# Eight early pairs of MLP blocks instead of four, their two first products kept in DRAM instead of PSUM

## The chip, the cores and the metric

The kernel runs on one core of one Trainium2 chip. TensorE (PE in the profile) multiplies, VectorE (DVE), ScalarE (ACT) and GpSimd (POOL) work element by element, and SyncE (SP) here only issues DMAs; ACT and POOL issue DMAs too. Each engine works through its own queue in the order in which the built program has it. The metric is the device time of one execution in microseconds (us). A kernel is run several times, and the median counts; beside it there is one profiled execution, from which all rows below come.

## The reference

The program is one layer of a decoder on 512 tokens of width 2048, in float32: a norm, a token mixer of four kinds of heads, a residual, a second norm, and a squared-ReLU MLP with a hidden width of 8192, a residual, and a last norm. The change is in the second norm and in the first half of the MLP:

```python
def _sq_relu_mlp(h, w_up, w_down):
    return jnp.square(jax.nn.relu(h @ w_up)) @ w_down

    for l in range(DEPTH):
        ...
        m = _rmsnorm(h, norm2_w[l])
        h = h + _sq_relu_mlp(m, w_ffn_up[l], w_ffn_down[l])
    return _rmsnorm(h, final_norm_w)
```

## The kernel before

**Precision.** A float32 operand is split into two parts (`hi`, cast to fp32r on ACT, and `lo`, the rest, subtracted on DVE), and a product is three matmuls: hi by hi, hi by lo, lo by hi. In `product` these are lines L1440, L1441 and L1442, eight times over (k = 0 to 7), 24 matmuls of 256 columns.

**The up product.** `m @ w_up` is done with a Strassen-Winograd scheme of seven products in place of eight. The activations are cut into four quarters (tokens by width), of which seven operands are made: `a11`, `a12`, `s1`, `s2`, `s3`, `s4`, `a22` (each as hi and lo, transposed). The weights are cut into 64 blocks of 128 columns, which are taken in 32 pairs. For each pair p, four pieces of 512 KB ("11", "21", "12", "22") are loaded by `load_pair`, summed as the scheme wants it (L1431), split (L1433 on ACT, L1434 on DVE, both in `prepare`), multiplied (`product`), and the seven results are put together by `combine` into a tile `ct` of eight parts, which ACT writes to DRAM as one DMA of 1 MB (L1607, `hq`, called h in the rows). There are two `ct` tiles, so the tile of pair p + 2 is the one of pair p, and its first write waits until the 1 MB of pair p has landed. `prepare` runs three products ahead of PE, and `load_pair` two pairs ahead.

**The second norm and the early products.** The operands `a11` and `a12` belong to the first half of the tokens and are there first. The other five need the norm of the second half, which DVE computes (L391, L1368 and on), and PE transposes what comes out (L1337, four transposes to a "turn", 20 turns). In that stretch PE also runs products 1 and 2 (`a11` with "11", `a12` with "21") of the first EARLY = 4 pairs: eight products, in the loop over `j`, with the 20 turns dealt out among them by `step`. `norm_second` is a generator; a `yield n` lets n steps pass, and there are eight steps to a product. Product 1 of the early pairs stays in two PSUM banks (`X`), the square of the ReLU of products 1 + 2 goes to DRAM through POOL (`e11`, L1490). The weights of these eight products are loaded and split apart from the pairs' own (L287, L280, L281), so that the early pairs' "11" and "21" are loaded twice.

**The order.** From the second norm to the end of the up product, the queues of PE and POOL are in program order, as written. The order of the other queues (DVE, ACT, SP) is set by a planner that places an instruction where it expects its inputs to be ready. `units` is the list of products after the early ones: five for an early pair (products 5, 6, 7, 3, 4), seven for any other. Every seventh unit lets POOL issue three DMAs that add weights of the down product in DRAM (L309, L310, L312, L314, tile t); that is spaced by a small copy on ACT (L309).

Of the kernel before, what the change touches and what calls it, by code (L numbers as in the profile page):

```python
# [191 lines left out]
def tile_trunk(ctx: ExitStack, tc: tile.TileContext, ins, out):  # L192
    nc = tc.nc
    V, A, PE, G = nc.vector, nc.scalar, nc.tensor, nc.gpsimd
    pool = lambda name, bufs, **kw: ctx.enter_context(tc.tile_pool(name=name, bufs=bufs, **kw))
    cp = pool("c", 1)
# [42 lines left out]

        return 8 * (p // 4) + p % 4, 8 * (p // 4) + 4 + p % 4  # L240

    EARLY = 4
    hq = [pd.tile([128, 8, 4, 256], F32, tag=f"h1_{c}", name=f"h1_{c}") for c in range(8)]
    e11 = [pd.tile([128, 256], F32, tag=f"e{p}", name=f"e{p}") for p in range(EARLY)]
    seq = [(ins["win"][b, q], 8 * len(BLOCKS[b])) for b in range(NBLK) for q in range(2)]
    seq += [(ins["wout"][n, q], 1024) for n in range(4) for q in (6, 7, 0, 1)]
    seq += 2 * [(ins["wout"][n, q], 1024) for n in range(4) for q in (4, 5, 2, 3)]
# [1108 lines left out]
    def norm_second(ss):  # L1356

        pairs = [(tt, c) for tt in range(2) for c in range(2)]
        for t in (2, 3):
            spill(t)  # L1360
        rs = [mean_rsqrt(None, ss[tt]) for tt in range(2)]
        for tt in range(2):
            for i in range(4):
                norm_i(ht[2 + tt], rs[tt], nrow2, ht[2 + tt], i)
        a11, a12, a21, a22 = ({p: ht[2 * i + p[0]][2 * j + p[1]] for p in pairs} for i in range(2) for j in range(2))
        s1 = {p: R("s1") for p in pairs}
        for p in pairs:
            V.tensor_tensor(s1[p], a21[p], a22[p], op=ALU.subtract)  # L1368
        yield 30
        for p in pairs:  # L1370
            turn("s1", s1[p], *p)
            yield 2
        ready.add("s1")
        s2 = {p: S("s2") if p in pairs[:2] else a11[p] for p in pairs}
        for p in pairs[2:]:
            V.tensor_tensor(a21[p], a11[p], a21[p], op=ALU.subtract)
        for p in pairs:
            V.tensor_tensor(s2[p], s1[p], a11[p], op=ALU.subtract)
        for p in pairs:
            yield 2  # L1380
            turn("s2", s2[p], *p)
        ready.add("s2")
        for p in pairs:
            V.tensor_tensor(a12[p], a12[p], s2[p], op=ALU.add)
        for p in pairs:
            yield 2
            turn("s4", a12[p], *p)
        for p in pairs[:2]:
            V.tensor_tensor(a21[p], a11[p], a21[p], op=ALU.subtract)
        for p in pairs:  # L1390
            yield 2
            turn("s3", a21[p], *p)
        for p in pairs:
            turn("a22", a22[p], *p)

    def pass2(th):
# [46 lines left out]
            if between:  # L1443
                between()

    def xbank(p):
        if p < EARLY:
            if p % 2 == 0:
                bank["e"] = pp.tile([128, 512], F32, tag="pp", name="x")
            return bank["e"][:, 256 * (p % 2):256 * (p % 2) + 256]  # L1450
        return pp.tile([128, 512], F32, tag="pp", name="x")[:, 0:256]

    in_order(EN.PE, EN.Pool)
    ss = pass2(0)
    operand("a11", AT)
# [11 lines left out]
        operand(name, home)  # L1467
    todo.append([norm_second(ss), 1])
    step()
    X = {}  # L1470
    ct0 = cp.tile([128, 512], F32, name="ct0")
    for j in range(2 * EARLY):
        p, m = j // 2, 1 + j % 2
        h, l = weights(2)
        if j == 2 * EARLY - 3:
            load_pair(0)
        if j >= 2 * EARLY - 3:
            prepare(j + 3 - 2 * EARLY)
# [12 lines left out]

# [74 lines left out]

    post, cts = [], {}

    def combine(p, m, acc):


        if p not in cts:
            cts[p] = pu.tile([128, 8, 256], F32, tag="ct", name="ct", bufs=2)
            if p < EARLY:
                A.copy(cts[p][:, 2], X[p])
        ct = cts[p]
        if m == 1:
            A.copy(ct[:, 2], acc)  # L1580
        elif m == 2:
            x = cts[p, 2] = pu.tile([128, 256], F32, tag="c11", name="c11", bufs=2)
            V.tensor_tensor(x, ct[:, 2], acc, op=ALU.add)
        elif m == 5:
            A.copy(ct[:, 5], acc)
        elif m == 6:
            V.tensor_tensor(ct[:, 0], ct[:, 2], acc, op=ALU.add)
# [21 lines left out]
    for u, (p, m) in enumerate(units):  # L1609
# [143 lines left out]
```

## Time and profile before

| what | us |
|---|---|
| median of 3 runs (lowest, highest) | 2385.65 (2385.21, 2393.04) |
| the profiled execution, time | 2385.64 |
| its span, first to last instruction | 2383.8 |
| PE busy in it | 2319.7 (97%) |
| DVE busy | 1773.7 (74%) |
| ACT busy | 1016.8 (43%) |
| first matmul of the early products (L1440, tile x) | 1075.3 |
| first matmul of the units (L1440, tile p) | 1120.1 |

In the rows below a time is in us from the start of the span. A row of a timeline has start, length, engine, line, operation, out<-in, how many, and in brackets how long the engine sat idle before it and what ended that. Matmuls are pipelined, so that their lengths overlap; the distance between starts is what counts. The same holds for DVE and ACT, where the next instruction starts a little before the one ahead has ended. A row of the view by stretches has the length, then busy time and count of PE, of PE's weight loads, DVE, ACT and POOL, then the granted TensorE clock, the share of the DMA engines, and GB/s.

### The profile page before, as it was taken

What the parts mean: (1) busy time and instruction counts of PE and PEld (TensorE: products, weight loads), DVE (VectorE), ACT (ScalarE), POOL (GpSimd) and SP (SyncE); (2) the same over time, 40 slices, a digit from 0 to 9 for tenths busy, and PEclk for the clock granted to TensorE, in tenths of its full rate; (3) what the DMA queues carried; (4) which work ended last, traced back from release to release, by engine and by line L of the source; (5) the groups of instructions that cost most, each with busy time, mean ns of one, the idle gap of its engine ahead of it and who ended that gap; (6) DMA issues with size and microseconds to landing.
All of it is one profiled execution on the core that took longest, in us unless ns stands there. A gap on an engine that the chain in (4) does not pass through costs nothing.

```text
span 2383.8 us, 36706 instructions
## 1 busy us (share of the span) xinstructions
PE 2319.7 (97%) x14690; PEld 1988.4 (83%) x14690; DVE 1773.7 (74%) x2783; ACT 1016.8 (43%) x1480; POOL 193.1 (8%) x270
## 2 busy tenths in 40 slices
PE   6999999999999999998999999999989999999996
PEld 6777778777777788877999999999978888888885
DVE  5685855775584444468888888888868888898898
ACT  5323233323322232354555555555555444444443
POOL 1110201211210210011011000000010000000000
PEclk9999999999999999999999999999999999999998
DMA  5553626564653676465877754445385655656451
GB/s 198 146 142 82 163 71 153 154 147 107 164 145 91 181 193 226 148 223 175 249 221 208 217 175 138 157 158 176 115 325 176 212 161 175 201 181 207 160 196 71
DMA packets 159915, 404.76 MB, mean 170 GB/s; under 512 B 12928, under 2 KB 79488, under 8 KB 158720
## 3 DMA queue, kind: packets, MB, share of 16 engines
q1 hardware_dynamic: 83952, 285.42, 36.7%
q0 software_dynamic: 38912, 77.08, 14.3%
q10 hardware_dynamic: 36880, 39.92, 4.9%
q8 instruction: 115, 1.88, 0.3%
q14 instruction: 56, 0.46, 0.1%
HBM read 355.70 MB, written 113.77 MB: 197 GB/s over the span
## 4 chain that ended last, share of the span: by engine, by line
PE 78%; DVE 10%; issue 6%; DMA 3%; POOL 1%; ACT 1%; SPq 0%; POOLq 0%; ACTq 0%; DVEq 0%
PE acc L456 17%; PE dn L1659 8%; PE dn L1658 8%; PE dn L1657 8%; PE p L1440 8%; PE p L1442 8%; PE p L1441 8%; PE wo L1238 2%; PE wo L1239 2%; PE wo L1246 2%; DVE lo L281 1%; PE acc L480 1%; DVE lo L1563 1%; DVE lo L1434 1%; DVE xi L566 1%
## 5 line engine op out<-in xcount | busy, mean ns | idle before, releaser
L1657 PE MATMUL dn<-hi,x 128*128 128x512 f32 x896 | 351.6, 392 | 11.2 <-ACT hi L1562 9.1
L1562 ACT CAST hi<-raw 128x1024 fp32r<-128x1024 f32 x224 | 235.5, 1054 | 294.9 <-PE dn L1659 233.9
L1658 PE MATMUL dn<-lo,x 128*128 128x512 f32 x896 | 351.6, 392 | 3.3 <-DVE lo L1563 3.1
L1659 PE MATMUL dn<-hi,x 128*128 128x512 f32 x896 | 351.4, 392 | 0.5 <-DVE x L1563 0.5
L280 ACT CAST hi<-raw 128x1024 fp32r<-128x1024 f32 x162 | 169.9, 1049 | 406.8 <-PE acc L456 307.2
L456 PE MATMUL acc<-ah,hi 128*128 128x512 f32 x832 | 336.4, 404 | 0.0
L456 PE MATMUL acc<-al,hi 128*128 128x512 f32 x832 | 335.4, 403 | 0.0
L456 PE MATMUL acc<-ah,lo 128*128 128x512 f32 x832 | 333.8, 401 | 0.0
L1563 DVE TENSOR_TENSOR lo<-raw,hi 128x1024 fp32r<-128x1024 f32 x224 | 272.7, 1221 | 65.7 <-ACT hi L1562 64.9
L1433 ACT CAST hi<-raw 128x1024 fp32r<-128x1024 f32 x216 | 226.3, 1050 | 209.3 <-PE p L1441 146.6
L1434 DVE TENSOR_TENSOR lo<-raw,hi 128x1024 fp32r<-128x1024 f32 x216 | 262.6, 1220 | 68.4 <-ACT hi L1433 67.8
L281 DVE TENSOR_TENSOR lo<-raw,hi 128x1024 fp32r<-128x1024 f32 x160 | 195.2, 1221 | 144.7 <-ACT hi L280 129.2
L1657 PEld LDWEIGHTS dn<-hi,x 128*128 128x128 f32 x896 | 169.7, 189 | 48.3 <-ACT hi L1562 10.4
L1658 PEld LDWEIGHTS dn<-lo,x 128*128 128x128 f32 x896 | 169.6, 189 | 40.2 <-DVE lo L1563 5.0
L1659 PEld LDWEIGHTS dn<-hi,x 128*128 128x128 f32 x896 | 169.7, 189 | 36.3 <-DVE x L1563 1.0
L456 PEld LDWEIGHTS acc<-ah,hi 128*128 128x128 f32 x832 | 156.3, 188 | 38.4 <-issue 7.4
L456 PEld LDWEIGHTS acc<-ah,lo 128*128 128x128 f32 x832 | 156.4, 188 | 34.6 <-issue 2.9
L456 PEld LDWEIGHTS acc<-al,hi 128*128 128x128 f32 x832 | 156.5, 188 | 32.0 <-issue 1.9
L1431 DVE TENSOR_TENSOR raw<-raw,raw 128x1024 f32<-128x1024 f32 x124 | 151.4, 1221 | 4.3 <-DMA raw<-in_wup_dram 2.6
L1558 DVE TENSOR_TENSOR raw<-raw 128x1024 f32<-128x1024 f32 x64 | 77.7, 1220 | 3.7 <-DMA raw<-in_wdn_dram 3.1
L310 POOL TENSOR_TENSOR pace<-pace,mhalf 128x1 f32<-128x1 f32 x64 | 37.7, 589 | 446.8 <-ACT pace L309 446.7
L1563 DVE TENSOR_TENSOR x<-raw,x 128x1024 fp32r<-128x1024 f32 x56 | 68.1, 1218 | 6.8 <-ACT x L1562 6.8
(498 smaller groups left out, 5057.2 us busy)
## 6 DMA issues: line engine op xcount, KB each, us to landing
raw<-in_wup_dram SPq DMA_DIRECT2D x136, 512.0 KB, 5.7
t<-in_wdn_dram POOLq DMA_DIRECT2D x128, 512.0 KB, 8.0
raw<-in_win_dram SPq DMA_DIRECT2D x106, 512.0 KB, 3.8
raw<-in_wdn_dram SPq DMA_DIRECT2D x96, 512.0 KB, 4.5
h<-ct ACTq DMA_DIRECT2D x32, 1024.0 KB, 9.5
raw<-t SPq DMA_DIRECT2D x64, 512.0 KB, 4.4
raw<-h SPq DMA_DIRECT2D x56, 512.0 KB, 3.9
raw<-in_wout_dram SPq DMA_DIRECT2D x48, 512.0 KB, 4.1
```

The source lines that it names most:

```text
L281: by.tensor_tensor(l[:, :w], r[:, :w], h[:, :w].bitcast(F32), op=ALU.subtract)
L456: PE.matmul(acc[:w], a, b, start=n == 0, stop=n == 47)
L1433: A.copy(h, r)
L1434: V.tensor_tensor(l, r, h.bitcast(F32), op=ALU.subtract)
L1440: PE.matmul(acc, wh, rh[:, k], start=k == 0, stop=False)
L1441: PE.matmul(acc, wh, rl[:, k], start=False, stop=False)
L1442: PE.matmul(acc, wl, rh[:, k], start=False, stop=k == 7)
L1562: A.copy(h, r[1])
L1563: V.tensor_tensor(l, r[1], h.bitcast(F32), op=ALU.subtract)
L1657: PE.matmul(accs[t], xh, h[:, ws], start=kk == 0, stop=False)
L1658: PE.matmul(accs[t], xh, l[:, ws], start=False, stop=False)
L1659: PE.matmul(accs[t], xl, h[:, ws], start=False, stop=kk == 3)
```

## The change

EARLY goes from 4 to 8: 16 products in place of 8 run among the turns of the second norm, and pairs 4 to 7 have five units in place of seven. The numbers in `norm_second` are set so that its 20 turns are dealt out over 16 products (36, then 3 between turns, 6 more ahead of each new operand).

Product 1 of the early pairs is no longer kept in PSUM: ACT copies it to a tile `e0` and writes it to DRAM; product 2 is added to it, squared and written behind it (`e1`), both by DMAs that ACT issues (16 of 128 KB, where POOL issued 4). In the units, `early_of(p)` loads both halves back with one DMA of 256 KB on SP into a tile `c11` of which there is one; it is called for pair 0 ahead of the first loads and for pair p + 1 in the `combine` of product 7 of pair p. Product 6 takes its first half from there, and an ACT copy puts the second half into `ct` (L1592 of the changed kernel). The ACT copy out of PSUM at the begin of an early pair (L1577 before) is gone.

```diff
-    EARLY = 4
+    EARLY = 8
-    e11 = [pd.tile([128, 256], F32, tag=f"e{p}", name=f"e{p}") for p in range(EARLY)]
+    e11 = [pd.tile([128, 512], F32, tag=f"e{p}", name=f"e{p}") for p in range(EARLY)]
...
-        yield 30
+        yield 36
         for p in pairs:
             turn("s1", s1[p], *p)
-            yield 2
+            yield 3
...
+        yield 6
         for p in pairs:
-            yield 2
+            yield 3
             turn("s2", s2[p], *p)
...
+        acc = (BK("p") if m == 1 else pp.tile([128, 512], F32, tag="pp", name="z"))[:, 0:256]
+        product(acc, m, h, l, step)
         if m == 1:
-            X[p] = xbank(p)
-            product(X[p], 1, h, l, step)
-            c11 = ct0[:, 256 * (p % 2):256 * (p % 2) + 256]
-            A.copy(c11, X[p])
+            e0 = cp.tile([128, 256], F32, tag="e0", name="e0")
+            A.copy(e0, acc)
+            nc.scalar.dma_start(e11[p][:, 0:256], e0)
         else:
-            z = BK("z")[:, 0:256]
-            product(z, 2, h, l, step)
-            V.tensor_tensor(c11, c11, z, op=ALU.add)
-            A.activation(c11, c11, AF.Relu)
-            A.activation(c11, c11, AF.Square)
-            G.dma_start(e11[p], c11)
+            e1 = cp.tile([128, 256], F32, tag="e1", name="e1")
+            V.tensor_tensor(e1, e0, acc, op=ALU.add)
+            A.activation(e1, e1, AF.Relu)
+            A.activation(e1, e1, AF.Square)
+            nc.scalar.dma_start(e11[p][:, 256:512], e1)
...
+    def early_of(p):
+        if (p, 2) not in cts:
+            cts[p, 2] = pu.tile([128, 512], F32, tag="c11", name="c11", bufs=1)
+            nc.sync.dma_start(cts[p, 2], e11[p])
+        return cts[p, 2]
+
     def combine(p, m, acc):
         if p not in cts:
             cts[p] = pu.tile([128, 8, 256], F32, tag="ct", name="ct", bufs=2)
-            if p < EARLY:
-                A.copy(cts[p][:, 2], X[p])
...
         elif m == 6:
-            V.tensor_tensor(ct[:, 0], ct[:, 2], acc, op=ALU.add)
+            V.tensor_tensor(ct[:, 0], ct[:, 2] if p >= EARLY else early_of(p)[:, 0:256], acc, op=ALU.add)
         elif m == 7:
...
             if p < EARLY:
-                nc.sync.dma_start(ct[:, 2], e11[p])
+                A.copy(ct[:, 2], cts[p, 2][:, 256:512])
+                if p + 1 < EARLY:
+                    early_of(p + 1)
```

The planner sets ACT's queue anew. Before, at the crossing from pair 2 to pair 3, from the write of h of pair 1 to that of pair 2 (L1433 are casts of weights for products to come, L1577 is the first write to the `ct` of pair 3, which waits for the write of pair 1 to land; L1598 to L1603 finish pair 2):

```order
L1607 DMA h_0_81<-ct 1024x1x256
L1433 CAST hi<-raw_10481 128x1024
L1433 CAST hi<-raw_10485 128x1024
L1577 COPY ct<-x 128x256
L1598 ACTIVATE ct<-ct 128x2x256
L1599 ACTIVATE ct<-ct 128x2x256
L1433 CAST hi<-raw_10487 128x1024
L1602 ACTIVATE ct<-ct 128x256
L309 COPY pace<-hi 128x1
L1603 ACTIVATE ct<-ct 128x256
L1433 CAST hi<-raw_10481 128x1024
L1607 DMA h_0_81<-ct 1024x1x256
```

With the change, the same place from the first write to the `ct` of pair 3 (now L1592) to the write of h of pair 2 (L1609); the write of pair 1 stands two rows ahead of the first row, with one cast between:

```order
L1592 COPY ct<-c_11028 128x256
L1437 CAST hi<-raw_10784 128x1024
L1437 CAST hi<-raw_10780 128x1024
L1600 ACTIVATE ct<-ct 128x2x256
L1437 CAST hi<-raw_10786 128x1024
L1601 ACTIVATE ct<-ct 128x2x256
L309 COPY pace<-hi 128x1
L1604 ACTIVATE ct<-ct 128x256
L1605 ACTIVATE ct<-ct 128x256
L1585 COPY ct<-p 128x256
L1437 CAST hi<-raw_10780 128x1024
L1609 DMA h_0_81<-ct 1024x1x256
```

Ahead of the waiting copy there is now one cast since the last write of h, and two casts of pair 3's weights (products 7 and 6) that were ahead of it stand behind it. The same pattern, with two casts behind, is at pair 4; at pair 5 it is the cast for product 6; at pairs 6 and 7 the cast of the fourth product (3) is the first behind it.

In the second norm DVE's queue changes as well. Before, from the last sum for `s2` (L1378) to the first halves of `s4`, with L336 the `lo` part of a turn, L1384 sums for `s4`, L1431 and L1434 for the first units:

```order
L1378 TENSOR_TENSOR h_1_8555<-s_9813,h_1_8555 128x512
L1431 TENSOR_TENSOR raw<-raw 128x1024
L336 TENSOR_TENSOR s2l<-bk,s2h 128x4x128
L1384 TENSOR_TENSOR h_2_8552<-h_2_8552,s_10013 128x512
L1434 TENSOR_TENSOR lo<-raw,hi 128x1024
L336 TENSOR_TENSOR s2l<-bk,s2h 128x4x128 x3
L1384 TENSOR_TENSOR h_3_8553<-h_3_8553,s_10014 128x512
L1384 TENSOR_TENSOR h_2_8556<-h_2_8556,h_0_8554 128x512
L1384 TENSOR_TENSOR h_3_8557<-h_3_8557,h_1_8555 128x512
L336 TENSOR_TENSOR s4l<-bk,s4h 128x4x128
```

And with the change, with L281 the `lo` part of an early product's weights and L1482 the sum of products 1 and 2:

```order
L1378 TENSOR_TENSOR h_1_8559<-s_9817,h_1_8559 128x512
L1482 TENSOR_TENSOR e_10075<-e_10019,z 128x256
L281 TENSOR_TENSOR lo<-raw,hi 128x1024 x2
L336 TENSOR_TENSOR s2l<-bk,s2h 128x4x128 x3
L1482 TENSOR_TENSOR e_10166<-e_10111,z 128x256
L281 TENSOR_TENSOR lo<-raw,hi 128x1024
L336 TENSOR_TENSOR s2l<-bk,s2h 128x4x128
L1385 TENSOR_TENSOR h_2_8556<-h_2_8556,s_10067 128x512
L1385 TENSOR_TENSOR h_3_8557<-h_3_8557,s_10068 128x512
L1385 TENSOR_TENSOR h_2_8560<-h_2_8560,h_0_8558 128x512
L1385 TENSOR_TENSOR h_3_8561<-h_3_8561,h_1_8559 128x512
L336 TENSOR_TENSOR s4l<-bk,s4h 128x4x128 x2
```

The splits and sums of the eight added early products stand among the work of the norm, and the preparation of the first units has moved behind it.

More of the change, by code (lines that the diff above doesn't have):

```diff
@@ L1384, in norm_second @@
             V.tensor_tensor(a12[p], a12[p], s2[p], op=ALU.add)
+        yield 6
         for p in pairs:
-            yield 2
+            yield 3
             turn("s4", a12[p], *p)
@@ L1389, in norm_second @@
             V.tensor_tensor(a21[p], a11[p], a21[p], op=ALU.subtract)
+        yield 6
         for p in pairs:
-            yield 2
+            yield 3
             turn("s3", a21[p], *p)
         for p in pairs:
+            yield 3
             turn("a22", a22[p], *p)
@@ L1444, in product @@
                 between()
-    def xbank(p):
-        if p < EARLY:
[L1448 to L1451, printed above, removed]
     in_order(EN.PE, EN.Pool)
@@ L1469, in tile_trunk @@
     step()
-    X = {}
-    ct0 = cp.tile([128, 512], F32, name="ct0")
     for j in range(2 * EARLY):
@@ L1575, in combine @@
             cts[p] = pu.tile([128, 8, 256], F32, tag="ct", name="ct", bufs=2)
-            if p < EARLY:
-                A.copy(cts[p][:, 2], X[p])
         ct = cts[p]
@@ L1581, in combine @@
         elif m == 2:
-            x = cts[p, 2] = pu.tile([128, 256], F32, tag="c11", name="c11", bufs=2)
-            V.tensor_tensor(x, ct[:, 2], acc, op=ALU.add)
+            x = cts[p, 2] = pu.tile([128, 512], F32, tag="c11", name="c11", bufs=1)
+            V.tensor_tensor(x[:, 256:512], ct[:, 2], acc, op=ALU.add)
         elif m == 5:
@@ L1591, in combine @@
             if p < EARLY:
-                nc.sync.dma_start(ct[:, 2], e11[p])
+                A.copy(ct[:, 2], cts[p, 2][:, 256:512])
+                if p + 1 < EARLY:
+                    early_of(p + 1)
             else:
-                A.activation(ct[:, 2], cts[p, 2], AF.Relu)
+                A.activation(ct[:, 2], cts[p, 2][:, 256:512], AF.Relu)
                 A.activation(ct[:, 2], ct[:, 2], AF.Square)
@@ L1617, in tile_trunk @@
             RW = lambda n: pu.tile([128, 1024], F32, tag="r2", name=n, bufs=6)
+            early_of(0)
             load_pair(1)
```

## The prediction

> **What bounds the kernel now.** I read the page's shares first, then the waits of PE, then a table by stretches of the part that the change touches.
>
> ```profile
> PE 2319.7 (97%) x14690; PEld 1988.4 (83%) x14690; DVE 1773.7 (74%) x2783; ACT 1016.8 (43%) x1480; POOL 193.1 (8%) x270
> PE 78%; DVE 10%; issue 6%; DMA 3%; POOL 1%; ACT 1%; SPq 0%; POOLq 0%; ACTq 0%; DVEq 0%
> ```
>
> PE is the bound, and no matmul is removed: what the change can win is PE's waiting around the second norm. The stretches are the eight early products, the four early pairs of five products, and two pairs of seven, cut at each pair's first product:
>
> ```profile
> 1075.30:1120.10 44.80, 34.21 (x273) 32.99 (x272) 41.61 (x63) 22.96 (x43) 5.42 (x10) 0.96 0.38 125
> 1120.10:1134.40 14.30, 14.30 (x123) 14.30 (x122) 11.98 (x15) 6.76 (x12) 2.34 (x4) 1.00 1.03 343
> 1134.40:1148.70 14.30, 14.30 (x123) 14.30 (x122) 13.15 (x18) 6.76 (x10) 0.00 (x0) 1.00 0.90 286
> 1148.70:1162.90 14.20, 14.20 (x121) 14.20 (x121) 13.97 (x18) 7.67 (x13) 2.02 (x3) 1.00 0.72 206
> 1162.90:1178.20 15.30, 14.56 (x123) 14.37 (x122) 8.99 (x13) 6.45 (x11) 2.29 (x3) 1.00 0.79 251
> 1178.20:1198.70 20.50, 20.26 (x170) 20.06 (x169) 19.68 (x24) 11.58 (x17) 2.60 (x3) 1.00 0.91 278
> 1198.70:1218.70 20.00, 20.00 (x170) 20.00 (x169) 18.37 (x24) 11.68 (x18) 2.59 (x3) 1.00 0.75 211
> ```
>
> In the first row PE idles 44.80 - 34.21 = 10.6 us while DVE works 41.61 of 44.80. In the pairs of five DVE is nearly full too (13.97 of 14.20 in pair 2), in pair 3 it falls to 8.99 of 15.30, and there PE loses 0.74 us, then 0.24. A pair of seven takes 20.0 us, 2.86 a product, and PE does not wait. PE's waits from 1040 to 1200 us:
>
> ```profile
> PE bk L1337 <- DVE s L1378: 4.6, 1, 4.6
> PE bk L1337 <- DVE h L1389: 3.5, 1, 3.5
> PE bk L1337 <- DVE s L1368: 1.9, 1, 1.9
> PE p L1442 <- DVE lo L1434: 1.0, 2, 0.7
> ```
>
> Three of the four are turns that wait for DVE's sums; the last is a product that waits for its weights. The first three the change goes after; the last is the one to watch.
>
> **The early stretch.** Sixteen products in place of eight, and the same 20 turns:
>
> ```profile
> 1075.34 0.28 PE L1440 MATMUL x<-a11h,hi 128*128 128x256 f32 x1
> 1078.21 0.28 PE L1440 MATMUL z<-a12h,hi 128*128 128x256 f32 x1
> 1090.50 0.60 PE L1337 MATMUL bk<-ident,s 128*128 128x128 f32 x4
> 1091.64 0.60 PE L1337 MATMUL bk<-ident,s 128*128 128x128 f32 x4
> ```
>
> A product is 2.87 us, so a step is 0.36; from turn to turn with two steps between it is 1.14, so a turn is 0.42. Without a wait the new stretch is 16 x 2.87 + 20 x 0.42 = 54.3 us, to 1129.6. Before, it was 44.8 us and the eight moved products came later for 8 x 2.86 = 22.9, together 67.7. **At most 13.4 us can be won** (the 10.6 of waiting, 4% of 44.8 for the granted clock of 0.96, and a little that overlaps).
>
> DVE says how much of it comes. Its queue from the last L1368 on, with distances from start to start:
>
> ```profile
> 1087.41 2.49 DVE L1368 TENSOR_TENSOR s<-h,h 128x512 f32<-128x512 f32 x4
> 1096.29 1.28 DVE L1376 TENSOR_TENSOR h<-h,h 128x512 f32<-128x512 f32 x2
> 1097.49 1.28 DVE L1378 TENSOR_TENSOR s<-s,h 128x512 f32<-128x512 f32 x2
> 1127.98 0.41 DVE L1587 TENSOR_TENSOR ct<-ct,p 128x256 f32<-128x256 f32 x1
> 1128.31 1.22 DVE L1431 TENSOR_TENSOR raw<-raw,raw 128x1024 f32<-128x1024 f32 x1
> 1129.45 1.22 DVE L1434 TENSOR_TENSOR lo<-raw,hi 128x1024 fp32r<-128x1024 f32 x1
> ```
>
> That is 0.60 for a sum or a lo part of 512 columns, 0.33 for one of 256, 1.13 for one of 1024 (I use these for all of a size). In the new order there follow 11 lo parts of early weights (12.4), 20 of turns (12.0), 7 sums L1482 (2.3), 12 sums of the norm (7.2), 3 additions and 3 lo parts for the first units (6.8): 40.7 us from 1089.9, to 1130.6. So DVE ends 1 us behind what PE could do, with next to no slack between them. ACT gets 8 more casts (0.95 each, from the row of 1170.28 below to the one after it: 7.6), 4 more triples of copy, ReLU and square (0.27 + 2 x 0.33, taken as DVE's: 3.7), and 16 DMA issues:
>
> ```profile
> L1209 ACTq DMA_DIRECT2D ol<-o x8: 327/416/646, 811.4 to 814.8; - x8
> ```
>
> at 0.42, 6.7 us: 23 + 18 = 41 of 55, hidden, but in the same chain (turn, cast, lo part). I take the first unit at 1132, 1130.6 to 1135. Against 1120.1 + 22.9 = 1143.0 that **wins 11 us** (8 to 13.4). The eight weight loads and the e writes fall into a stretch with a DMA share of 0.38; the four POOL DMAs and the PSUM copies that go were not waited for. At nothing, too.
>
> A rule of the Trainium skill bears on the size of it: TensorE: Matmul & The Clock Gate, "HAM oscillation", asks for no idle gap of PE over some 3.4 us, since after one the array runs at half clock again. The trace agrees in direction: the stretch with gaps of 4.6 and 3.5 has 0.96, the others 1.00. By the rule each new wait over 3.4 us would also cost about half a window, 1.7 us, by estimate.
>
> **The pairs of five.** Eight in a row in place of four. What held pair 3 was ACT:
>
> ```profile
> 1142.69 0.60 ACTq L1607 DMA_DIRECT2D h<-ct  x1
> 1151.36 0.37 ACT L1577 COPY ct<-x 128x256 f32<-128x256 f32 x1 [2.35 <-DMA h<-ct]
> 1157.66 0.56 ACTq L1607 DMA_DIRECT2D h<-ct  x1
> 1168.81 0.37 ACT L1577 COPY ct<-x 128x256 f32<-128x256 f32 x1 [6.41 <-DMA h<-ct]
> 1169.08 0.63 ACT L1598 ACTIVATE ct<-ct 128x512 f32<-128x512 f32 x1
> 1170.28 1.04 ACT L1433 CAST hi<-raw 128x1024 fp32r<-128x1024 f32 x1
> 1171.23 0.41 ACT L1602 ACTIVATE ct<-ct 128x256 f32<-128x256 f32 x1
> 1174.18 0.52 ACTq L1607 DMA_DIRECT2D h<-ct  x1
> 1186.71 0.37 ACT L1580 COPY ct<-p 128x256 f32<-128x256 f32 x1 [0.98 <-DMA h<-ct]
> ```
>
> The first write into a `ct` waits until the 1 MB of two pairs ago has landed: 8.7, 11.1 and 12.5 us after issue. All of ACT stands behind it, the casts of the next weights and the end of the pair before (L1598 to L1603), then DVE behind ACT. Before, two casts for pair 3 had gone ahead of the copy, and PE lost only 0.74. The changed kernel still has such a copy (L1592), for every early pair, and at pairs 3 and 4 the planner has put those casts behind it.
>
> So there is a loop. Let the copy start at X. Until the next write of h is issued: copy 0.27, cast 0.95, on DVE two lo parts 2.26, L1603 0.33, a lo part 1.13, L1606 0.60, an addition 1.13, and on ACT the cast that needs it 0.95: 7.6 us (before, with fewer rows between, 6.3 and 5.4 by the rows above). Then the landing, then the next copy. With 11.1 us, the median of the three, a turn of the loop is 18.7 us, while PE has 14.3 us of products for it:
>
> - Pair 3: if X is where L1577 was, 5.9 us into the pair, product 6 gets its lo part at 5.9 + 0.27 + 0.95 + 2.26 = 9.4, wanted at 2.86 + 0.24: 6.3 us. X moves with two landings; both at 8.7 take off 2.4, the load of `c11` with it may add as much. I take 5.5 (2 to 9).
> - Pairs 4 and 5: 18.7 - 14.3 = 4.4 each, 8.8 (landings of 8.7 and 12.5: 4 to 11.6).
> - Pairs 6 and 7: the first cast behind the copy is the fourth product's, two products more of slack (5.7), which the loop uses up in little more than a pair. I take 1.5 (0 to 6).
>
> Sum 15.8, less the 0.98 that pairs 3 and 4 lost before: **14.8 us lost**. From pair 8 on the pairs have seven products, 20.0 us to a loop of 18.7, and it closes. The load of `c11` goes out once DVE has read the one before (L1587), and lands in
>
> ```profile
> raw<-in_wup_dram SPq DMA_DIRECT2D x19, 512.0 KB, 7.1
> t<-in_wdn_dram POOLq DMA_DIRECT2D x6, 512.0 KB, 8.9
> h<-ct ACTq DMA_DIRECT2D x3, 1024.0 KB, 11.1
> ct<-e SPq DMA_DIRECT2D x4, 128.0 KB, 8.0
> ```
>
> some 8 us (median from 1120 to 1180 us, for half the size): the same copy waits for it, but L1587 is 9.2 us after X, so that its loop is 9.5 + 8 = 17.5, just under that of h. Loads of weights for pair p + 2 go out with the third to fifth split of pair p, as before; SP has the `c11` load ahead of some, which waits for less than they do. That the DMAs share the engines with the additions of t is in the landings.
>
> **Sum.** 2385.65 - 11 + 14.8 = 2389.5. The profiled execution (2385.64, span 2383.8) is at the median, so nothing is to be scaled.
>
> **The rivals.**
> 1. *The wait isn't there.* The copy was hoisted before too, and pairs 1 and 2 lost nothing; if h lands in 6.7 us or less, the loop fits into 14.3, and the win stands: 2385.65 - 11 - 1 = 2374, 2372 to 2377. For it: a minimum of 4.6 over all 32 writes; against it: none of the three in this stretch, at a DMA share of 0.72 to 1.03.
>
> ```profile
> DMA to landing us min/median/max: 4.6/9.5/16.3
> ```
>
> SBUF — State Buffer of the Trainium skill, "The DMA setup-cost knee", gives 2 us + bytes / 436 GB/s, which for 1 MB is 4.4 us, an estimate; by that this rival would hold and the time would be near 2374. The trace disagrees where it matters: 8.7 to 12.5 us with weights and t in flight.
>
> 2. *The wait rules*, slower by over half a per cent: the copy on L309 stands beside L1609, so that three DMAs of t run into the write of h. At 14 us (max 16.3) the loop is 21.6: pairs 4 and 5 lose 7.3 each, pair 3 nine, 6 and 7 five, 28 - 1 - 11 = +16, 2402. It decides from a landing of about 13.
> 3. *The early stretch doesn't win*: DVE and ACT in turn hold the first unit until 1140, 3 us won; with the 14.8, 2397. Against it: DVE's list is 40.7 us long by count, and most of it has no input that comes late.
>
> **How the numbers follow.** Half a per cent, 12 us (2373.7 and 2397.6), is about what a measurement tells from no change here. My forecast, both terms and a small sum, 2383 to 2397: 0.50. Rival 1: 0.22, of which 0.06 lies under 2373.7. Rival 2: 0.18. Rival 3: 0.10, half of it over 2397.6. So faster 0.06, slower 0.18 + 0.05 = 0.23, same 0.71. The range takes in the forecast, most of rival 1 and half of rival 2: 2374 to 2402.
>
> **What would show it.** In the profile after: the first L1440 of tile p at 1132 (1130.6 to 1135), PE's waits for L1378 and L1389 (now L1391) gone or under 1 us, and DVE over 95% busy from 1090 on. Then ACT's L1592 with idle of some us ahead of it put down to a DMA, PE waiting at the second product (L1442, for a lo part) of pairs 3, 4 and 5, and starts of pairs 3 to 6 at distances of 17 to 20 us in place of 14.3. If the pairs keep 14.3 us, rival 1 holds; if PE waits for turns as before, rival 3. I am wrong altogether if PE waits at a place that the change does not touch, such as the step from the up to the down product.

## The result, and the profile after

The changed kernel takes **2399.89 us** (median of 5 runs, 2396.47 to 2404.0), the kernel before, in 5 runs, 2385.21. The ratio is 1.0059 (95% interval 1.0046 to 1.0072): slower by 0.6%, 10 us over the forecast of 2389.5 and inside the range. The profiled execution has a span of 2396.0 us, 12.2 more than before. In the experiments further down, one execution of pool_sums (3785.76 us) and one of pool_sums_copy (7968.72 us) stand far above all others, and the ratios are taken without them.

By stretches (the same view and columns as in the prediction): the early stretch in two parts, then pairs 3, 4 and 5.

```profile
1075.85:1090.00 14.15, 14.15 (x120) 14.14 (x119) 12.55 (x22) 6.90 (x13) 3.74 (x7) 1.00 0.63 212
1090.00:1136.67 46.67, 42.51 (x348) 42.16 (x347) 39.50 (x55) 28.64 (x51) 0.00 (x0) 0.96 0.61 191
1179.53:1200.97 21.44, 16.49 (x122) 16.29 (x121) 17.07 (x21) 7.58 (x12) 2.33 (x3) 0.84 0.71 210
1200.97:1222.44 21.47, 16.71 (x123) 16.21 (x121) 13.98 (x17) 7.58 (x12) 1.75 (x3) 0.84 0.70 232
1222.44:1244.97 22.53, 17.50 (x122) 17.09 (x121) 17.10 (x21) 9.46 (x13) 0.00 (x0) 0.85 0.67 189
```

The early stretch is 1136.67 - 1075.85 = 60.8 us long. Before, stretch and the eight products that moved into it were 44.8 + 22.9 = 67.7: **6.9 us won**. Pairs 0 to 2, 6 and 7 keep their 14.3 us, but pairs 3, 4 and 5 take 21.4, 21.5 and 22.5. The eight pairs together take 136.8 us; before, pairs 0 to 7 less the moved products took 138.7 - 22.9 = 115.8: **21.1 us lost**. The first early product starts 0.5 later, with the same instructions ahead of it. After pair 7 the span is 2.5 shorter than before. 0.5 - 6.9 + 21.1 - 2.5 = 12.2.

What became shorter lies at the step from the up to the down product. The 61.2 us from 1738.80 on hold 221 matmuls before, at a granted clock of 0.92; the same length from the same point of the program on (1753.50) holds 231 after, at 0.94. No run isolates this, and its cause stays open.

Now the waits of PE in the changed stretch:

```profile
PE p L1444 <- ACT hi L1437: 8.4, 2, 4.3
PE p L1446 <- DVE lo L1438: 6.4, 3, 4.9
PE bk L1337 <- DVE h L1385: 2.8, 1, 2.8
PE bk L1337 <- DVE s L1378: 1.4, 1, 1.4
```

And what ACT and DVE stood at in pairs 3 to 5 (timeline; in brackets the idle time ahead and what ended it):

```profile
1184.94 0.40 ACT L1592 COPY ct<-c 128x256 f32<-128x256 f32 x1 [8.42 <-DMA h<-ct]
1205.76 0.41 ACT L1592 COPY ct<-c 128x256 f32<-128x256 f32 x1 [10.90 <-DMA h<-ct]
1223.55 0.41 ACT L1592 COPY ct<-c 128x256 f32<-128x256 f32 x1 [8.13 <-DMA h<-ct]
...
1172.32 0.72 SPq L1425 DMA_DIRECT2D raw<-in_wup_dram  x1
1180.50 1.23 DVE L1435 TENSOR_TENSOR raw<-raw,raw 128x1024 f32<-128x1024 f32 x1 [5.34 <-DMA raw<-in_wup_dram]
1203.02 2.36 DVE L1435 TENSOR_TENSOR raw<-raw,raw 128x1024 f32<-128x1024 f32 x2 [4.64 <-DMA raw<-in_wup_dram]
1226.19 2.36 DVE L1435 TENSOR_TENSOR raw<-raw,raw 128x1024 f32<-128x1024 f32 x2 [6.95 <-DMA raw<-in_wup_dram]
```

The copy L1592 waits for the write of h, as the prediction said, 8 to 11 us each time. But DVE stands as well, at a *sum of weights* (L1435), which waits for loads that went out 8 to 10.5 us before: the one at 1180.5 needs two pieces, and the later of them went out at 1172.32 and landed 8.1 us after. PE in pair 3 first misses the lo part of product 5, which is behind this sum on DVE; its cast was done at 1176.5, ahead of ACT's wait:

```profile
1184.88 0.58 PE L1446 MATMUL p<-s1h,lo 128*128 128x256 f32 x1 [4.95 <-DVE lo L1438]
1208.11 0.58 PE L1444 MATMUL p<-s2h,hi 128*128 128x256 f32 x1 [4.11 <-ACT hi L1437]
1229.74 0.39 PE L1444 MATMUL p<-s2h,hi 128*128 128x256 f32 x1 [4.28 <-ACT hi L1437]
```

DVE's queue, as the planner has it at this place, shows why (the four rows from DVE's first wait on; raw_10780 is a piece of pair 3, raw_10955 and raw_10959 are pieces of pair 4):

```
L1435 TENSOR_TENSOR raw_10955<-raw_10955,raw_10959 128x1024
L1435 TENSOR_TENSOR raw_10959<-raw_10959,raw_10961 128x1024
L1589 TENSOR_TENSOR ct<-ct,p 128x256
L1438 TENSOR_TENSOR lo<-raw_10780,hi 128x1024
```

The first sums of pair 4 stand *ahead of the first lo part of pair 3*, which PE wants a whole pair sooner. At pairs 4 and 5 one of the two sums stands ahead of the first lo part, the other ahead of the sum for product 6, and PE misses the cast of product 6, which needs this sum and stands behind ACT's copy as well. So two queues had each an instruction placed early that waits for a transfer, and both waits ended within 5 us of each other: DVE's at 1180.5 to 1182.1 and ACT's at 1184.9, then 1203.0 and 1205.8, then 1226.2 and 1223.6. The experiments take them apart.

### The profile page after: what moved, and what is told of

It reads as the page before. It is cut to its first block, busy times and chain, and to the rows that moved or that the text cites. A ratio compares the mean times of both kernels' runs of the same rounds, so it can differ in the third digit from the quotient of the medians.

```text
span 2396.0 us, 36760 instructions
## 1 busy us (share of the span) xinstructions
PE 2323.2 (97%) x14690; PEld 1993.7 (83%) x14690; DVE 1774.2 (74%) x2783; ACT 1016.6 (42%) x1484; POOL 192.4 (8%) x266
## 3 DMA queue, kind: packets, MB, share of 16 engines
q0 software_dynamic: 38720, 76.56, 14.2%
## 4 chain that ended last, share of the span: by engine, by line
PE 79%; DVE 9%; issue 6%; DMA 3%; POOL 1%; ACT 1%; SPq 0%; POOLq 0%; DVEq 0%; ACTq 0%
PE acc L456 17%; PE p L1446 8%; PE p L1444 8%; PE p L1445 8%; PE dn L1661 8%; PE dn L1662 8%; PE dn L1660 8%; PE wo L1238 2%; PE wo L1246 2%; PE wo L1239 2%; DVE lo L281 1%; PE acc L480 1%; DVE lo L1558 1%; DMA raw<-in_wup_dram 1%; DVE xi L566 1%
## 5 line engine op out<-in xcount | busy, mean ns | idle before, releaser
L281 DVE TENSOR_TENSOR lo<-raw,hi 128x1024 fp32r<-128x1024 f32 x168 | 204.9, 1223 | 145.9 <-ACT hi L280 126.4
L1435 DVE TENSOR_TENSOR raw<-raw,raw 128x1024 f32<-128x1024 f32 x124 | 151.3, 1222 | 19.4 <-DMA raw<-in_wup_dram 17.9
L1444 PE MATMUL p<-s2h,hi 128*128 128x256 f32 x256 | 74.5, 291 | 8.4 <-ACT hi L1437 8.4
```

The lines of the kernel that those rows point to most:

```text
L281: by.tensor_tensor(l[:, :w], r[:, :w], h[:, :w].bitcast(F32), op=ALU.subtract)
L1444: PE.matmul(acc, wh, rh[:, k], start=k == 0, stop=False)
```

## The experiments

Each kernel is the changed one with the edits shown. The ratio is to the kernel before as it ran beside that kernel (medians of 2384.5 to 2388.3). A run's early stretch, from its one profiled execution, is the time from its first early product to its first unit, and the loss is what its pairs of five take over 14.27 us each (1.0 in the kernel before, all in pair 3). These are compared, and not the spans: the first early product started anywhere from 1074.6 to 1079.3 in these profiles, with the same code ahead of it.

| run | median, us | ratio to before (95%) | early stretch | pairs of five, us | loss |
|---|---|---|---|---|---|
| changed kernel | 2399.89 | 1.0059 (1.0046 to 1.0072) | 60.8 | 14.3 14.3 14.3 21.4 21.5 22.5 14.3 14.3 | 22.7 |
| pool_copy | 2396.36 | 1.0049 (1.0033 to 1.0065) | 61.1 | 14.3 14.3 14.3 21.9 21.0 20.6 14.3 14.3 | 20.8 |
| e1_two | 2392.84 | 1.0032 (1.002 to 1.0045) | 56.9 | 17.8 18.5 14.3 14.3 16.6 22.3 14.3 14.3 | 18.2 |
| both_edits | 2384.58 | 0.9998 (0.9987 to 1.0009) | 57.4 | 15.3 17.8 14.3 14.3 15.6 21.0 14.3 14.3 | 12.7 |
| four_in_dram | 2385.68 | 1.0001 (0.9991 to 1.0011) | 46.8 (8 products) | 14.3 14.3 14.3 14.3 | 0 |
| pool_sums | 2412.41 | 1.0104 (1.0089 to 1.0119) | 60.8 | 14.3 14.7 20.8 19.5 23.1 21.4 14.7 21.8 | 36.0 |
| pool_sums_copy | 2387.68 | 1.0008 (0.9999 to 1.0017) | 61.5 | 14.3 14.3 15.3 17.9 16.9 15.5 16.5 14.4 | 10.9 |
| three_edits | 2385.41 | 0.9997 (0.9988 to 1.0006) | 57.2 | 14.3 14.3 16.7 20.0 15.1 15.3 16.5 14.4 | 12.5 |
| t_later | 2388.26 | 1.0013 (1.0003 to 1.0022) | 63.1 | 14.3 14.3 14.3 17.5 19.3 16.0 14.3 14.3 | 10.0 |
| as_written | 2400.73 | 1.0051 (1.0037 to 1.0065) | 62.5 | 14.3 14.3 18.9 18.3 16.8 19.8 16.8 15.7 | 20.8 |
| as_written_e1 | 2397.74 | 1.0041 (1.0029 to 1.0054) | 56.7 | 14.3 14.3 19.5 18.3 16.8 19.8 18.3 14.3 | 21.3 |
| as_written_e1_t | 2396.64 | 1.0035 (1.0022 to 1.0047) | 56.8 | 14.3 14.3 17.8 19.9 18.3 17.1 19.8 14.2 | 21.4 |
| six_pairs | 2375.31 | 0.9962 (0.995 to 0.9974) | 47.4 (12 products) | 14.3 14.3 14.3 14.3 14.3 14.3 | 0 |

### The storage alone

EARLY back at 4 and the turns dealt out as before; products 1 and 2 still go through `e0`, `e1` and DRAM.

```diff
-    EARLY = 8
+    EARLY = 4
```

> Only the storage is changed: EARLY is 4 and the turns are dealt out as before, but products 1 and 2 go through e0, e1 and DRAM as in the changed kernel. Theory (the loss comes from eight pairs of five units in a row, the DRAM scheme by itself costs little, as the loop of copy and write has only pairs 2 and 3 to build up): 2387 us (2384 to 2391), the pair with the copy that waits longest loses at most 5 us. Rival (the storage in DRAM is the cause): over 2393.

Measured 2385.68, no difference to before. No pair loses anything. The early stretch is 2.0 us longer than the 44.8 before. So the storage in DRAM is not the cause by itself.

### The copy that waits for h

```diff
-                A.copy(ct[:, 2], cts[p, 2][:, 256:512])
+                G.tensor_copy(ct[:, 2], cts[p, 2][:, 256:512])
```

> One edit: the copy of the second half of c11 into ct (L1592) is made by POOL, whose queue is in program order, in place of ACT, whose queue the planner orders. Theory (the wait of that copy for the write of h holds up ACT, and the casts behind it): pairs 3, 4 and 5, now 21.4, 21.5 and 22.5 us, come down to 14.3 to 16; PE loses less than 3 us from 1136 to 1275 in place of 14.8 of waiting and 7.8 of slower clock; the first unit stays at 1136.7; the time is 2378 us (2375 to 2383). Rival (two ct tiles are too few with a landing of 10 us, wherever the first write into one stands): the wait moves to the copy of product 5 (L1585), the pairs stay at 17 to 20 us, and the time stays over 2392.

Measured 2396.36, with pairs 3 to 5 as long as ever. The theory is wrong, and of the rival only the time came true: ACT no longer waits for h anywhere, not at L1585 either (of its waits from 1130 to 1260 the longest in all, 48.1 us, is for DVE's sums, and none is for a transfer), and the pairs still take 21 us. What holds them is DVE's wait for loads:

```profile
1183.18 1.23 DVE L1435 TENSOR_TENSOR raw<-raw,raw 128x1024 f32<-128x1024 f32 x1 [7.06 <-DMA raw<-in_wup_dram]
1206.21 2.36 DVE L1435 TENSOR_TENSOR raw<-raw,raw 128x1024 f32<-128x1024 f32 x2 [4.92 <-DMA raw<-in_wup_dram]
```

So the wait that the prediction named was real and, alone, worth 22.7 - 20.8 = 1.9 us; a second one beside it holds the same products. In the changed kernel ACT's wait had ended after DVE's in pairs 3 and 4 only, and in pair 3 the part that PE missed did not stand behind it.

### The write of e1

```diff
-            e1 = cp.tile([128, 256], F32, tag="e1", name="e1")
+            e1 = cp.tile([128, 256], F32, tag="e1", name="e1") if p % 2 == 0 else (S if p == 1 else R)("e1")[:, 0:256]
```

> One edit: e1 of pairs 1, 3, 5 and 7 is put into storage that is free by then (a tile of s for pair 1, of n for the others), so that the sum of products 1 and 2 (L1482) no longer waits for the write of the pair before to land. Theory (that wait, 1.2 and 2.2 us of DVE's time, is what kept the early stretch from ending at 1132): L1482 has no idle time put down to a DMA, PE's waits for L1378 and L1385 (1.4 and 2.8 us) fall under 1 us each, the first unit is at 1132 to 1133.5; the pairs behind it as in the changed kernel; the time is 2396 us. Rival (DVE's list itself is too long): DVE is busy over 95% from 1090 on, and the first unit stays within 1 us of 1136.7; the time is 2400.

In the changed kernel DVE waits for the write of `e1` of the pair before, of which there is one tile; the view is that of DVE's waits:

```profile
DVE e L1482 <- DMA e<-e: 4.7, 3, 2.2
```

With two the early stretch is 56.9 us in place of 60.8, 3.9 shorter, and PE's two waits there go from 1.4 and 2.8 to 0.4 and 1.4. This theory holds for the stretch: nearly all of what was missing of the 11 us was the turn of `e1`, not the length of DVE's list. The pairs changed too: pairs 0 and 1 now lose 3.5 and 4.3. The load of `c11` for pair 0 goes out at 1136.48, 4.2 us after the first unit (in the changed kernel at 1125.04, 11.6 ahead of it), with loads of weights behind it, and DVE waits for both:

```profile
1142.41 0.42 DVE L1587 TENSOR_TENSOR ct<-c,p 128x256 f32<-128x256 f32 x1 [4.84 <-DMA c<-e]
1147.69 1.23 DVE L1435 TENSOR_TENSOR raw<-raw,raw 128x1024 f32<-128x1024 f32 x1 [3.53 <-DMA raw<-in_wup_dram]
```

Another 2.3 and 8.0 are lost in pairs 4 and 5. In this edit the last `e1` lies in storage that the tiles of the pairs take over; in three_edits and as_written_e1, where it does not, pairs 0 and 1 lose nothing. That this is what delayed the loads is argued from there, since these two have other edits as well.

### Both

> The POOL copy and the second storage for e1 together. Theory: the two gains add up, first unit at 1132 to 1133.5, pairs of 14.3 to 16 us, time 2374 us (2371 to 2380), 0.3 to 0.6% under the kernel before. Rival for the copy: over 2388. Rival for the early stretch: 2378, as with the POOL copy alone.

Measured 2384.58, like the kernel before and 10 us over the theory's 2374. The early stretch has its gain (57.4), the pairs lose 12.7 (4.6 of it in pairs 0 and 1, where DVE waits 4.9 us for `c11` as in e1_two), and DVE waits 9.6 us in all for loads of weights.

### The sums that wait for loads

The sums for products 5 and 7 of pairs 2 to 7 go to POOL (pool_sums); then this and the copy on POOL (pool_sums_copy); then also a second storage for `e1` in pairs 1, 3, 5 and 6 (three_edits).

```diff
-            V.tensor_tensor(r, r, rw[p, b], op=ALU.add)
+            (G if m in (5, 7) and 1 < p < EARLY else V).tensor_tensor(r, r, rw[p, b], op=ALU.add)
```

> The changed kernel with one edit: in pairs 2 to 7 the sums for products 5 and 7 (L1435, of pieces 11 with 12, and 12 with 22) are made by POOL. In the changed kernel the planner puts these two sums of pair p + 1 on DVE ahead of the first lo part of pair p, and DVE waits there 5 to 7 us for loads of pair p + 1 that were issued 8 to 11 us before (1180.5, 1203.0, 1226.2). Theory (two waits end at the same time, DVE's for these loads and ACT's for the write of h, and either alone holds the pairs): without DVE's wait, L1592 on ACT still waits 6 to 11 us, pairs 3 to 5 stay at 18 to 21 us, the time is 2390 to 2399 us. Rival (DVE's wait is the one that counts): the pairs fall to 14.3 to 16, the time to 2380.

> The sums for products 5 and 7 of pairs 2 to 7 and the copy L1592 on POOL, so that neither ACT nor DVE stands behind a transfer that is a pair early. Theory (two coinciding waits): pairs 3 to 5 at 14.3 to 16 us in place of 21.4 to 22.5, no idle of DVE over 2 us put down to a load of w_up, first unit at 1136.7, time 2378 us (2375 to 2384). Rival (the DMA engines cannot bring what a pair of five needs in 14.3 us, wherever it is waited for: 2 MB of weights, 1 MB of h, 0.25 MB of c11 and the additions of t, at a share of 0.7 to 1.0 now): the pairs stay over 17 us, PE waits for casts whose sums wait on POOL, and the time is over 2388.

> The sums and the copy on POOL, and a second storage for e1 (pairs 1, 3, 5 and 6, so that the last one is back in the old tile and the tiles that come after are free early). Theory: first unit at 1132 to 1133.5 and pairs of 14.3 to 16 us: 2374 us (2371 to 2379), 0.25 to 0.6% under the kernel before. Rival (DMA engines): 2384 as with the two edits before, since pairs that start earlier wait longer for the same loads.

pool_sums: 2412.41, slower than either theory had it. DVE is free of loads, ACT waits 31.6 us for h, and the pairs lose 36.0. That the other wait alone holds the pairs is borne out: PE's long waits there are for casts that stand right behind the copy. Its size is not: POOL, whose sums wait 28.9 us for loads, is a new wait in the chain, and no run shows what part of the added loss is due to it.

pool_sums_copy: 2387.68, a loss of 10.9 in place of 22.7. Neither ACT nor DVE stands long behind a transfer any more (DVE 1.3 us in all for loads). The theory's 14.3 to 16 us is missed in pairs 3, 4 and 6. There DVE itself is slow; groups by shape from 1150 to 1250 us, here and in the changed kernel:

```profile
L1438 DVE TENSOR_TENSOR lo<-raw,hi 128x1024 fp32r<-128x1024 f32 x30 | 51.7, 1733 | 2.8 <-ACT hi L1437 2.4
L1435 POOL TENSOR_TENSOR raw<-raw,raw 128x1024 f32<-128x1024 f32 x12 | 34.7, 2890 | 14.1 <-DMA raw<-in_wup_dram 5.1 <-DVE ct L1589 4.8 <-DVE ct L1590 4.2
```

```profile
L1438 DVE TENSOR_TENSOR lo<-raw,hi 128x1024 fp32r<-128x1024 f32 x28 | 34.0, 1221 | 5.0 <-ACT hi L1437 5.0
```

A lo part takes 1.73 us on the mean in place of 1.22, and POOL needs 2.89 for a sum that DVE does in 1.22. Single rows of DVE, and of POOL beside it, show the form of it:

```profile
1182.20 3.37 POOL L1435 TENSOR_TENSOR raw<-raw,raw 128x1024 f32<-128x1024 f32 x1 [4.83 <-DVE ct L1589]
1183.23 2.90 DVE L1590 TENSOR_TENSOR ct<-ct 128x512 f32<-128x512 f32 x1
1198.07 0.69 DVE L1590 TENSOR_TENSOR ct<-ct 128x512 f32<-128x512 f32 x1
1198.81 2.40 POOL L1435 TENSOR_TENSOR raw<-raw,raw 128x1024 f32<-128x1024 f32 x1 [4.19 <-DVE ct L1590]
1198.88 3.41 DVE L1438 TENSOR_TENSOR lo<-raw,hi 128x1024 fp32r<-128x1024 f32 x1
```

The same instruction takes 0.69 alone and 2.90 where a sum on POOL had begun before it. It then ends 0.6 us after that sum, and the lo part ends 1.1 us after its own: each about its own length. DVE is then busy 17.39 of the 17.86 us of pair 3. three_edits adds the gain of the early stretch (57.2) and loses 12.5: 2385.41. Neither wait alone, taken away, won more than 1.9 us in the pairs, and both together halve the loss. This is what two coinciding waits give; the other half stays. The Trainium skill has this in SBUF — State Buffer, "SBUF: two separate sides": DVE and GpSimd lock each other out of a port pair that they share, for a whole instruction, if DVE has two inputs in SBUF. The rows agree. The expectations for these runs had not used it.

### The traffic

```diff
-        if u % 7 == 4:
+        if u >= 40 and u % 5 == 4:
```

> The changed kernel with the additions of t taken out of the eight early pairs: from unit 40 on every fifth unit in place of every seventh of all. Nothing else in the order of ACT and DVE moves. Theory (the waits are as long as the transfers, and the transfers are slow because t is in flight): h lands in 6 to 8 us in place of 8.5 to 12.5, the loads of w_up in 4 to 6 us, pairs 3 to 5 take 15 to 17 us, the first unit stays at 1136.7, the time is 2386 us (2381 to 2391). Rival (t does not matter for the landings): pairs 3 to 5 at 21 us, time 2400.

Measured 2388.26, a loss of 10.0 in place of 22.7, with ACT's and DVE's queues as in the changed kernel but for the place of the small copy L309. From 1130 to 1270 us, median landings here and in the changed kernel:

```profile
raw<-in_wup_dram SPq DMA_DIRECT2D x38, 512.0 KB, 4.5
h<-ct ACTq DMA_DIRECT2D x8, 1024.0 KB, 8.5
```

```profile
raw<-in_wup_dram SPq DMA_DIRECT2D x37, 512.0 KB, 5.1
h<-ct ACTq DMA_DIRECT2D x7, 1024.0 KB, 10.0
```

Landings get shorter by 0.6 and 1.5 us, less than was expected, and DVE's waits for loads (L1435) from 1130 to 1260 us go from 17.9 to 11.7. That goes with 12.7 us, over half of the loss: where a queue stands behind a transfer in every pair, a microsecond of landing counts every time, and of the 7.9 us that PE is busy beyond its work in pairs 3 to 5 (worked out further down) 3.3 are left, with one stretch of 3.41 us at half clock in place of three of 6.83.

### The order as written

DVE and ACT in program order from unit 3 to unit 39; a lo part is written one product after its cast (as_written). Then with the second storage for `e1` (as_written_e1), then with t moved too (as_written_e1_t).

```diff
+        if u == 3:
+            in_order(EN.PE, EN.Pool, EN.DVE, EN.Activation)
+        if u == 5 * EARLY:
+            in_order(EN.PE, EN.Pool)
+        finish(u + 2)
...
-        prepare(u + 3)
+        prepare(u + 3, not 3 <= u < 5 * EARLY)
```

> The changed kernel with DVE and ACT in program order, as PE and POOL are, from unit 3 to unit 39 (the pairs of five), and planned everywhere else. To keep DVE from waiting for each cast, the lo part of a product is written one product after its sum and cast. So no sum stands a pair ahead of its use, and L1592 stands where its line is, behind product 7. Theory (the two hoisted instructions cost the pairs their 22 us, and the transfers themselves have time enough where nothing stands behind them early): all eight pairs at 14.3 to 15.5 us, first unit at 1136.7, time 2378 us (2375 to 2382). Rival (the DMA engines cannot bring what a pair of five needs in 14.3 us): the pairs from the third on still take 16 us or more, PE waits for lo parts whose sums wait for loads, time over 2385.

> The same, with the second storage for e1 in pairs 1, 3, 5 and 6. Theory: first unit 3 to 4 us earlier and pairs of 14.3 to 15.5 us: 2374 us (2371 to 2379), 0.25 to 0.6% under the kernel before. Rival (DMA engines): what starts earlier waits longer, 2383 or more.

> The same as the one before, and the additions of t moved out of the early pairs (from unit 40 on every fifth unit). Theory (queues, not transfers, set the pairs once the order is as written): within 3 us of the one before, about 2374. Rival (DMA engines): 5 to 10 us below the one before.

Measured 2400.73, 2397.74 and 2396.64; from the third on most pairs take 17 to 20 us, and 2378 and 2374 were wrong. But there is no wait for a transfer left to blame. DVE's waits from 1140 to 1250 us, and the landing of h (from 1130 to 1270 us), in as_written:

```profile
DVE lo L1447 <- ACT hi L1439: 11.9, 16, 0.8
DVE ct L1615 <- ACT ct L1614: 9.5, 6, 1.6
...
h<-ct ACTq DMA_DIRECT2D x7, 1024.0 KB, 5.8
```

h lands in 5.8 us, nobody waits for it, and DVE waits four times in each pair for ACT (0.8, 1.6, 0.6 and 0.8 us in pair 3, together 3.8). By the durations of the prediction DVE has 9 instructions of 1.13, 6 of 0.33 and 2 of 0.60 in a pair of five, 13.4 us. 13.4 + 3.8 = 17.2, and most pairs from the third on take 17 to 20, with some clock lost in them. **A pair of five leaves DVE 14.27 - 13.4 = 0.9 us.** That the planner's order covers these handovers is what it buys; this is argued from the waits, as the edit also moves the lo parts and the loads. Moving t is worth nothing here (a loss of 21.3 and of 21.4), so its worth in t_later came through the queues that stood behind transfers. The gain of `e1` in the early stretch is there again (62.5 to 56.7). What follows pair 7 takes 2.7 to 4.6 us longer in these three than in the changed kernel, and no run takes this apart.

### Six pairs

```diff
-    EARLY = 8
+    EARLY = 6
...
-        yield 36
+        yield 32
...
-            e1 = cp.tile([128, 256], F32, tag="e1", name="e1")
+            e1 = (S if p == 1 else R)("e1")[:, 0:256] if p in (1, 3, 4) else cp.tile([128, 256], F32, tag="e1", name="e1")
...
-        if u % 7 == 4:
+        if u >= 30 and u % 5 == 4:
```

> A version made to beat both: EARLY is 6, the turns are dealt out over 12 products (32, then 2 or 3 between turns, 4 more ahead of s2, s4 and s3), e1 of pairs 1, 3 and 4 in storage of its own, and the additions of t from unit 30 on, every fifth unit. Here the planner puts the first sum of pair p + 1 behind the first lo part of pair p, not ahead of it. Theory (DVE is nearly full in a pair of five and the early stretch, so fewer added products are hidden as well, and each of the waits behind a transfer is shorter by its share): first unit at about 1124, 7 us won of the 11.5 that four more early products are worth, the six pairs lose 0 to 4 us, 2381 us (2377 to 2386). Rival (pairs of five from the fourth on lose 3 to 5 us each whatever the order): pairs 3 to 5 at 17 to 19 us, 2387 or more.

Measured **2375.31**, ratio 0.9962 (0.995 to 0.9974): 0.4% under the kernel before and below the theory's range. All six pairs take 14.27 us:

```profile
1076.38:1123.74 47.36, 43.89 (x369) 43.22 (x368) 44.66 (x67) 28.80 (x52) 3.74 (x7) 1.00 0.54 174
1123.74:1209.36 85.62, 85.62 (x722) 85.62 (x721) 80.69 (x102) 44.96 (x65) 0.00 (x0) 1.00 0.79 263
```

Early stretch and the four moved products were 44.8 + 11.4 = 56.2 before and are 47.4 now: 8.9 won. In the pairs DVE does not wait for a load at all, and ACT's copy waits at most 2.5 us for h. Its DVE queue, at the place shown for the changed kernel (raw_10632 is a piece of pair 3, raw_10807 of pair 4):

```
L1438 TENSOR_TENSOR lo<-raw_10632,hi 128x1024
L1589 TENSOR_TENSOR ct<-ct,p 128x256
L1435 TENSOR_TENSOR raw_10632<-raw_10632,raw_10638 128x1024
L1590 TENSOR_TENSOR ct<-ct 128x2x256
L1435 TENSOR_TENSOR raw_10807<-raw_10807,raw_10811 128x1024
```

The first sum of pair 4 now stands behind the first lo part of pair 3 and behind pair 3's second sum. Which of the edits did it, the fewer pairs, t, or the other plan, no run takes apart; t alone left a loss of 10.0 with eight pairs, and eight pairs with both t and `e1` moved, in the planner's order, were not run.

## Why the prediction was right or wrong

**What bounds the kernel, and what can be won.** Right. PE's waits around the turns were what there was to win, and 13.4 us its limit.

**The early stretch, 11 us won.** 6.9. The count of instructions held: with the write of `e1` out of the way the stretch was 56.9 and 56.7 us, which is 10.8 and 11.0 won, and the first unit came at 1132.3 in e1_two. The step that failed is "The eight weight loads and the e writes" put "At nothing": the DMA engines had room (shares of 0.63 and 0.61), but `e1` is a ring of one, and DVE, with "next to no slack", stood in L1482 behind the writes, 3.3 us in the stretch and 4.7 in all. Where a buffer is single, its turn is a term of the sum. Rival 3 (the stretch wins 3) was as far off on the other side, and named another reason.

**The pairs of five, 14.8 us lost.** 21.1. The loop of copy and write was as predicted: from copy to the next write of h 8.3, 7.8, 13.6 and 7.0 us (7.6 predicted; in the 13.6 the cast behind the copy waits 4.7 us for DVE's sum), landings of about 10, 12.5, 10 and 8.5 (11.1). The waits of PE add up to 14.75 us, the three pairs in question 5.0, 4.8 and 5.0, where the prediction had 15.8, of which 1.5 in pairs 6 and 7, which lost nothing. But that agreement hides two faults.

First, the cause was only half of it. The step that failed is "Loads of weights for pair p + 2 go out with the third to fifth split of pair p, as before; SP has the `c11` load ahead of some, which waits for less than they do". I followed who issues the loads and not who waits for them. The planner had put both first sums of pair 4 ahead of the first lo part of pair 3 on DVE. Before, the first such sum (of pair 3) stood behind the first lo part of pair 2 and the other ahead of the second, and they hardly waited:

```profile
1144.24 1.23 DVE L1431 TENSOR_TENSOR raw<-raw,raw 128x1024 f32<-128x1024 f32 x1 [0.15 <-DMA raw<-in_wup_dram]
1148.53 1.23 DVE L1431 TENSOR_TENSOR raw<-raw,raw 128x1024 f32<-128x1024 f32 x1 [0.99 <-DMA raw<-in_wup_dram]
```

Their loads were 5.0 and 5.2 us old when DVE came to them, and took 5.0 and 6.2. In the changed kernel the load that the first sum of pair 4 needs was 2.8 us old (1172.32), and took 8.1. With ACT's wait gone (pool_copy) the pairs lose 20.8 of 22.7; with DVE's gone (pool_sums, where POOL's waits come in) they lose as much and more; with both gone, half is left. What part of that half is POOL in DVE's way and what DVE's own fullness these runs do not separate.

Second, the slower clock stood in a sentence by itself and not in the sum. In pairs 3 to 5 PE is busy 16.49, 16.71 and 17.50 us for work of 14.28: 7.9 us, a third of the loss. The trace has it in stretches of 6.83 us at half clock:

```profile
1182.58:1189.41 6.83, 4.53 (x21) 4.53 (x22) 6.83 (x9) 4.16 (x6) 0.00 (x0) 0.50 0.18 46
1206.47:1213.30 6.83, 4.54 (x19) 4.25 (x20) 6.12 (x8) 5.13 (x9) 0.00 (x0) 0.50 0.31 115
1230.37:1237.19 6.82, 6.19 (x29) 6.19 (x30) 6.58 (x9) 5.22 (x8) 0.00 (x0) 0.50 0.52 154
```

Half of the busy 4.53, 4.54 and 6.19 us is 7.6. The rule of the Trainium skill that the prediction cited (TensorE: Matmul & The Clock Gate, "HAM oscillation") gave 1.7 for each wait over 3.4 us, as an estimate; three such waits came, and 2.2, 2.4 and 3.2 us were paid. With 3 x 1.7 in the sum the forecast would have been near 2395.

**The sum.** 2389.5 + 4.1 (early stretch) + 6.3 (pairs) + 0.5 (ahead) - 2.5 (later) = 2397.9, which is the profiled execution (2397.74). The median lies 2.2 above it, within the spread of the five runs. Both terms missed to the same side.

**The rivals and the chances.** Rival 1, no wait, was wrong: for the copies of the pairs that lost, h landed in 10 to 12.5 us, not in 6.7. Rival 2, +16 from landings of 14 us, came within 3 us of the time with the wrong price: no such landing came. That the time lies inside the range is in part luck: its upper end was this rival's. "Same" had 0.71 and "slower" 0.23, with a bound at 2397.6; the median is 2.3 us beyond it. The mechanism that was missing, a second queue behind a transfer, works in one direction only, and a look at DVE's order in the pairs, and not in the norm alone, would have shown it.

**What would show it.** PE's wait for L1391 is gone, that for L1378 is 1.4 (under 1 was said), and a new one for L1385 has 2.8. The first unit was due at 1132 (to 1135) and came at 1136.7. DVE was to be over 95% busy from 1090 on: it was 39.50 of 46.67, 85%, which by itself said that a wait and not the list held the stretch. Starts at distances of 17 to 20 us were expected from pair 3 to pair 6; they were 21.4 to 22.5 for pairs 3 to 5. PE waited at the second product in pairs 4 and 5, for the cast first and then for the lo part, but at the first in pair 3, where ACT's copy had no part in it: there the second queue shows.

## What to carry to other kernels

Where a planner sets the order, look in every queue of the changed stretch for an instruction that waits for a transfer and stands ahead of work that is needed sooner; there may be two, and then taking away one wins next to nothing (1.9 of 22.7 us here). Count a single buffer that is written out by DMA as a loop with its own period, also where the DMA engines have room (a share of 0.61 here). More of a good thing has its limit: six early pairs, with t moved and a second storage for `e1`, win 0.4%, and eight as first built lose 0.6%. In a pair of five products DVE has 0.9 us left over, by count, and cannot make good a wait of several us.

## What the hardware showed

**The clock falls after shorter gaps than I had thought.** In pool_sums_copy PE's longest wait in pair 3 is 1.82 us. Two neighbouring stretches of 3.42 us there:

```profile
1185.77:1189.19 3.42, 1.59 (x14) 1.39 (x13) 3.32 (x5) 2.21 (x3) 0.94 (x1) 1.00 0.02 6
1189.19:1192.61 3.42, 3.42 (x18) 3.42 (x18) 3.42 (x4) 2.19 (x5) 2.54 (x4) 0.50 0.60 171
```

PE was busy 1.59 of 3.42 us, and the next 3.42 us run at half clock. But the wait of 3.54 us in the kernel before (for L1389, 1109.64 to 1113.18) cost no clock. Two stretches of 3.41 us, counted on from where the clock falls in that trace (1097.63), cut this wait in two:

```profile
1107.87:1111.28 3.41, 1.77 (x16) 1.56 (x14) 3.11 (x5) 2.95 (x6) 0.54 (x1) 1.00 0.10 41
1111.28:1114.69 3.41, 1.51 (x13) 1.54 (x14) 3.41 (x5) 0.59 (x1) 0.00 (x0) 1.00 0.00 0
```

Thirteen traces of this case have such a fall between 1040 and 1300 us. Of their stretches there, counted in this way, that ran at full clock, the clock stayed at 1.00 after each one with 1.79 us or less of idle PE, fell after each one with 1.96 or more, and fell after one of the six between. So in these traces the idle time within such a stretch decides, and not the length of a wait; the 3.4 us of idle time that the prediction went by is not what they follow.

**POOL can hold up DVE for the whole of an instruction**: 2.90 in place of 0.69 us for the same subtraction, while a POOL sum of 3.37 us runs beside it. Work that is moved from DVE to POOL in order to relieve DVE can leave it busier: 17.39 us in pair 3 of pool_sums_copy, where the fullest pair of five in the kernel before had 13.97.
